# Residual rows loaded into freed operand space, the order of seven products, and which bank is copied

## The chip, the core and the metric

One core of a Trainium2 chip runs the whole program; nothing is exchanged with other cores. The metric is device time in microseconds (us) of one execution. Engines are named as in the profile: PE does the matmuls, DVE and ACT the elementwise work, SP issues every DMA of the stages told of here, from one queue, in the order in which the issues stand.

## What is computed

A decoder block on x of 1024 tokens by 1024 channels, all float32: two token mixers in parallel (dilated attention and retention), their gated sum through an output projection, a residual add, and then the channel mixer, which is where most of the change lies:

```python
x = x + y @ w_out[l]
xn2 = rmsnorm(x, norm2_g[l])
x = x + jnp.square(jax.nn.relu(xn2 @ w_up[l])) @ w_down[l]
```

The up projection is 1024 by 4096, the down projection 4096 by 1024. The residual rows are the x of the second line, which the last line adds.

## The kernel before

**Split operands.** Every operand is held as a high and a low half (`split`, line 317: ACT rounds a copy to the high half, DVE subtracts it to get the low half), and each product of 128 by 128 by 512 is three matmuls: high by high, low by high, high by low (`Pipe.group`, line 218).

**Seven products.** The input projections, the up projection and the down projection use a seven-product scheme in the place of eight block products. The names N1 to N7 stand for the seven products. Several add up in one PSUM bank: N1 and N2 in bank "a", N6, N7 and N4 in bank "b" (which ACT first fills with minus the result of N1), N5 and N3 in bank "d" (`BANK`, line 253). A product of the up projection is 12 matmuls, one of the down projection 6.

**Order of the up projection.** `strassen_order` (line 256) writes the order out. In a unit j (256 of the 4096 columns) it is N6, N5, then N1 of unit j+2, N7, N2 of unit j+2, N4, N3; the last three units have less of j+2 in them. Because N7 and N4 add to the same bank, what N7 left there has to be read before N4 starts. `product` (line 368) does that: after N7, ACT copies bank b into the tile u3 (line 395), DVE subtracts bank d from it (line 396), and u3 is the block's result. After N3, DVE subtracts from bank d what ACT had copied after N6 (line 401).

**What becomes of the results.** `result` (line 1099) applies Relu and Square on ACT, forms four more sums on DVE (line 1116), and `put_operand` (line 1121) splits each of the seven operands of the down projection and writes it to DRAM (`h_d<-hs`, 512 KB each, seven in a unit, from four buffers). The weights of a unit come in two loads of 512 KB (`raw<-in_w_up`), are split into four pieces A to D, and a raw buffer is loaded again when its last piece has been split: the first of the two when piece B is (`wl2` or `wl3` in the names), the second when piece C is (`wl5`).

**The down projection.** Its units are (chunk c of 512 rows of w_down, pair t of token tiles), 32 in all, four to a chunk. `load_rows` (line 1135) brings a unit's seven operands from `h_d` into space that had held an operand of the up projection: two pieces, high and low, of 896 KB each; three units are in flight. `load_sums` (line 1145) loads the residual rows of two token tiles (Y, 512 KB each): Y0 and Y4 while the up projection still runs, the six others, Y1 to Y7, after it. `down` (line 1151) does one product of 6 matmuls, and DVE adds its bank to Y (line 1173). In a unit, N7 may start only when DVE has subtracted bank b, as N6 left it, from Y.

**Weights of a chunk.** Four loads of 512 KB (raw0 to raw3) into four buffers, then seven splits with four sums between them (`add_chunks`, line 137; the sums are line 153). In the even chunks they go to the weight buffers and the space of operand N2; in the odd chunks to buffer 3 and the space of the operands N7, N4 and N3.

**What sets the order.** PE runs in the order of the program. The instructions of the other engines are placed by a scheduler when the program is built, and each engine and the SP queue then run theirs strictly in that order: an instruction that waits holds up all behind it.

Of the kernel before, what the change touches and what calls it, by code (L numbers as in the profile page):

```python
# [10 lines left out]
F = mybir.dt.float32  # L11
# [257 lines left out]
def hybrid_block(ctx: ExitStack, tc: tile.TileContext, a: dict, out: bass.AP):  # L269
# [87 lines left out]
    for nb in range(2):  # L357
        for u in range(4):
# [2 lines left out]
    W.add_units("up", [a["w_up"][j] for j in range(NU)])  # L361
    NC = FF // 512
    W.add_chunks("dn", [[a["w_down"][c, i] for i in range(4)] for c in range(NC)],
                 [{"N1": 0, "N2": 1, "N3": 2, "N5": "N2a", "N7": "N2b", "N6": 5, "N4": 4},
                  {"N1": "N7a", "N2": "N7b", "N3": 3, "N5": "N4a", "N7": "N4b", "N6": "N3a", "N4": "N3b"}])
    pipe = Pipe(nc)

    def product(tag, j, name, unit, operands, pu, result):

        u = unit.setdefault(j, {})  # L370
        bank = BANK[name]
        fresh = bank not in u
# [12 lines left out]
        if name == "N1":  # L385
            u["b"] = ms.tile([P, 512], F, name="ms")
            nc.scalar.activation(u["b"], ps, AF.Copy, scale=-1.0)
        elif name == "N2":
            result(j, 0, lo, ps)
        elif name == "N6":  # L390
            u["u2"] = pu().tile([P, 512], F, name="u2")
            nc.scalar.activation(u["u2"], ps, AF.Copy)
        elif name == "N7":
            u["u3"] = pu().tile([P, 512], F, name="u3")
            nc.scalar.activation(u["u3"], ps, AF.Copy)  # L395
# [510 lines left out]
    with ExitStack() as ph:  # L906
# [15 lines left out]
            nc.sync.dma_start(t, src)  # L922
            return t

        ES, e1 = None, ExitStack()
        work = [(d, cs) for d in range(KT) for cs in halves()]
        gates = [loaded(pm2, sg_d[0, d, :, cs], "s0") for d, cs in work[:3]]
        waiting = [(place, n) for n, place in enumerate(oS)]
        for d in range(KT):
            ua, = W.take(1)  # L930
            uh, ul = W[ua]
            for cs in halves():
                if len(gates) < len(work):
                    e, es = work[len(gates)]
                    gates.append(loaded(pm2, sg_d[0, e, :, es], "s0"))
                sga = gates[2 * d + (cs.start > 0)]
                pp = ms.tile([P, 512], F, name="ms")
                pipe.step(pp, [(uh[:, k * P:(k + 1) * P], ul[:, k * P:(k + 1) * P], oaS[k][0][:, cs], oaS[k][1][:, cs])
                               for k in range(SLOTS)], {SLOTS - 1: lambda: W.free(ua)} if cs.start else None)
                nc.vector.tensor_tensor(sga, sga, pp, op=OP.mult)  # L940
                nc.sync.dma_start(pa_d[d, :, cs], sga)
                if ES is None and not pipe.due:
                    ret.close()
                    ext = pool(body, "ext", 3, "right")
# [46 lines left out]
        e1.close()  # L991


    W.more = pool(body, "more", 1, "right")
# [90 lines left out]
    with ExitStack() as ph:  # L1085
# [3 lines left out]
        def temps():  # L1089

            nonlocal up_pool
            if up_pool is None:
                assert pipe.slot > last_turn
                norm2.close()
                load_sums(pool(sumst, "y0", 1), 0)
                up_pool = pool(ph, "p26", 2)
            return up_pool

        def result(j, f, cs, src):
# [10 lines left out]
            held[j, q] = r  # L1110
            if q != "u2":
                put_operand(j, {"q11": "N1", "q12": "N2", "u3": "N4"}[q], r)
                return
            q11, q12, q21, q22 = (held.pop((j, q)) for q in ("q11", "q12", "u2", "u3"))
            for name, x, y in (("N5", q22, q21), ("N7", q21, q11), ("N6", q11, q22), ("N3", q12, q11)):
                nc.vector.tensor_tensor(x, x, y, op=OP.add)
                put_operand(j, name, x)

        held = {}

# [24 lines left out]
        def load_sums(from_, t):  # L1145

            for r in (t, t + 4):
                Y[r] = from_.tile([P, D], F, name=f"Y{r}")
                nc.sync.dma_start(Y[r], y_d[r * P:(r + 1) * P, :])

        def down(u, name):

# [26 lines left out]
        for j, name in strassen_order(NU):  # L1179
            product("up", j, name, unit, OP7, temps, result)  # L1180
            if j == NU - 1:
                if name == "N1":
                    load_rows(0)
                if name in ("N2", "N7", "N4", "N3"):
                    xh, xl = (x.rearrange("p a b -> p (a b)") for x in OP7[name])
                    for i, part in enumerate("ab"):
                        W.places[name + part] = xh[:, 1024 * i:1024 * i + 1024], xl[:, 1024 * i:1024 * i + 1024]
                    W.free(("place", name))
                if name == "N6":
                    load_rows(1)  # L1190
                if name == "N5":
                    load_rows(2)
                if name == "N7":
                    down(0, "N1")
                if name == "N4":
                    down(0, "N2")


    with ExitStack() as ph:
        y1 = pool(ph, "y1", 1)  # L1200
        for t in range(1, 4):
            load_sums(y1, t)
# [106 lines left out]
```

## Time and profile before

| | |
|---|---|
| median of 3 runs | 2282.35 us (2281.9 to 2283.52) |
| the profiled execution, its own time | 2283.06 us |
| its span, first to last instruction | 2281.3 us |
| granted PE clock, mean | 0.995 |
| PE busy in the span | 2230.9 us, 98% |
| DVE, ACT busy | 1340.2 us, 983.9 us |
| moved by DMA | 353.53 MB, 155 GB/s on average |

The up projection runs from about 1640 to 1963 us of the span, the down projection from there to the end, with a few products of each mixed at the seam. In the views, a row of a timeline is start, duration, engine, line, operation and, in brackets, how long the engine had been idle and what ended that. A line that says L223 is any matmul, L319 or L318 any split, so tile names tell more than lines: `wl<-raw,wh` is the split of a weight piece, `hs` that of an operand on its way to DRAM, `Y` a residual row tile. Names that begin with x (`xl<-raw,xh`) are weight pieces too, where they lie in space that had been an operand's.

### The profile page before, as it was taken

Reading aid. Unit: us, or ns where it says so; the run is one execution under the profiler, and the core shown is the slowest. Engines: PE = TensorE matmul, PEld = TensorE weight load, DVE = VectorE, ACT = ScalarE, POOL = GpSimd, SP = SyncE. Lnnn points to the kernel's source line nnn. Section 1 sums busy time; section 2 is a strip of 40 time slices with the busy share of each in tenths; the row PEclk is TensorE's granted clock in tenths of the full one; section 3 lists DMA queues with packets and bytes.
Section 4 is the critical chain, followed back from the end, with each engine's and each line's share of the span. In section 5 each row is a group of like instructions: output and inputs, shape, how many; then the busy total and the mean of one; then the engine's idle time right before and its main releaser. Section 6 shows DMA issues by size and latency. Waiting matters only on the chain.

```text
span 2281.3 us, 29992 instructions
## 1 busy us (share of the span) xinstructions
PE 2230.9 (98%) x10868; PEld 1910.0 (84%) x10868; DVE 1340.2 (59%) x2588; ACT 983.9 (43%) x2166; POOL 103.2 (5%) x148
## 2 busy tenths in 40 slices
PE   8999999999999999999999999999899999599999
PEld 7999999998888888878888888888787787488887
DVE  6444545355544445557777852453877777677774
ACT  6444435345333333435555633122666666322220
POOL 1111111110000000000000000000000000000000
PEclk9999999999999999999999999999999999799999
DMA  4313132222233333263433484564378889966655
GB/s 148 98 52 109 59 94 90 86 84 98 88 111 111 111 111 108 101 189 112 121 120 102 129 294 153 167 190 145 115 219 238 246 249 273 324 236 260 237 221 201
DMA packets 288805, 353.53 MB, mean 155 GB/s; under 512 B 14609, under 2 KB 215441, under 8 KB 288658
## 3 DMA queue, kind: packets, MB, share of 16 engines
q1 hardware_dynamic: 288658, 351.63, 48.5%
q8 instruction: 85, 1.39, 0.2%
q14 instruction: 62, 0.51, 0.1%
HBM read 229.84 MB, written 121.73 MB: 154 GB/s over the span
## 4 chain that ended last, share of the span: by engine, by line
PE 81%; DVE 6%; ACT 5%; DMA 4%; issue 3%; POOL 0%; SPq 0%; POOLq 0%; DVEq 0%; ACTq 0%
PE mm L223 53%; PE ms L223 22%; DMA raw<-in_w_up 2%; DVE wl L319 1%; PE ms L603 1%; PE ms L583 1%; ACT wh L318 1%; PE tr L659 1%; DVE xl L319 1%; ACT u L1108 1%; DVE hs L319 1%; ACT hs L318 1%; PE ms L596 1%; ACT u L1109 1%; PE ms L819 1%
## 5 line engine op out<-in xcount | busy, mean ns | idle before, releaser
L223 PE MATMUL mm<-wh,xh 128*128 128x384 f32 (+1 forms) x1280 | 502.9, 393 | 0.1
L319 DVE TENSOR_TENSOR wl<-raw,wh 128x1024 fp32r<-128x1024 f32 (+2 forms) x274 | 296.5, 1088 | 306.7 <-ACT wh L318 305.6
L223 PE MATMUL mm<-wh,xl 128*128 128x384 f32 (+1 forms) x1280 | 460.0, 359 | 2.3 <-DVE xl L319 2.3
L223 PE MATMUL mm<-wl,xh 128*128 128x384 f32 (+1 forms) x1280 | 459.0, 359 | 0.0
L318 ACT ACTIVATE wh<-raw 128x1024 fp32r<-128x1024 f32 (+2 forms) x274 | 258.5, 950 | 315.6 <-PE ms L223 75.2
L223 PE MATMUL mm<-xl,wh 128*128 128x512 f32 x848 | 309.3, 389 | 1.7 <-DVE xl L319 1.7
L223 PE MATMUL mm<-xh,wh 128*128 128x512 f32 x848 | 309.5, 389 | 0.0
L223 PE MATMUL mm<-xh,wl 128*128 128x512 f32 x720 | 280.1, 389 | 0.0
L223 PEld LDWEIGHTS mm<-wh,xl 128*128 128x128 f32 x1280 | 241.1, 188 | 24.7 <-DVE xl L319 3.3
L223 PEld LDWEIGHTS mm<-wh,xh 128*128 128x128 f32 x1280 | 242.1, 189 | 21.0 <-DVE Y L1173 0.6
L223 PEld LDWEIGHTS mm<-wl,xh 128*128 128x128 f32 x1280 | 243.0, 190 | 19.2 <-DVE wl L319 0.4
L223 PE MATMUL ms<-xh,wh 128*128 128x512 f32 x604 | 240.0, 397 | 6.5 <-ACT u L395 4.5
L223 PE MATMUL ms<-xl,wh 128*128 128x512 f32 x604 | 235.4, 390 | 0.7 <-DVE xl L319 0.7
L223 PE MATMUL ms<-xh,wl 128*128 128x512 f32 x604 | 235.3, 390 | 0.0
L223 PEld LDWEIGHTS mm<-xl,wh 128*128 128x128 f32 x848 | 159.2, 188 | 35.0 <-DVE xl L319 2.2
L223 PEld LDWEIGHTS mm<-xh,wh 128*128 128x128 f32 x848 | 159.2, 188 | 33.0
L223 PEld LDWEIGHTS mm<-xh,wl 128*128 128x128 f32 x720 | 135.1, 188 | 28.1
L223 PEld LDWEIGHTS ms<-xh,wh 128*128 128x128 f32 x604 | 113.5, 188 | 36.9 <-ACT u L395 10.5
L223 PEld LDWEIGHTS ms<-xh,wl 128*128 128x128 f32 x604 | 113.4, 188 | 24.0
L223 PEld LDWEIGHTS ms<-xl,wh 128*128 128x128 f32 x604 | 113.5, 188 | 22.9 <-DVE xl L319 1.0
L590 ACT ACTIVATE pr<-s,acc 128x128 f32<-128x128 f32 (+1 forms) x96 | 43.1, 449 | 148.6 <-DVE acc L588 122.1
L1173 DVE TENSOR_TENSOR Y<-Y,ms 128x512 f32<-128x512 f32 x96 | 65.8, 686 | 61.8 <-PE ms L223 61.7
(206 smaller groups left out, 3281.8 us busy)
## 6 DMA issues: line engine op xcount, KB each, us to landing
h_d<-hs SPq DMA_DIRECT2D x112, 512.0 KB, 5.2
xh<-h_d SPq DMA_DIRECT2D x32, 896.0 KB, 5.4
xl<-h_d SPq DMA_DIRECT2D x32, 896.0 KB, 7.1
raw<-in_w_att SPq DMA_DIRECT2D x48, 384.0 KB, 3.9
raw<-in_w_up SPq DMA_DIRECT2D x32, 512.0 KB, 4.3
raw<-in_w_down SPq DMA_DIRECT2D x32, 512.0 KB, 6.0
sg_d<-sg SPq DMA_DIRECT2D x32, 256.0 KB, 2.0
raw<-in_w_rqk_q SPq DMA_DIRECT2D x16, 512.0 KB, 3.7
```

The costliest lines, as they stand in the source:

```text
L223: self.nc.tensor.matmul(ps, x, y, start=start, stop=stop, skip_group_check=not first)
L318: nc.scalar.activation(dst_h, src, AF.Copy)
L319: nc.vector.tensor_tensor(dst_l, src, dst_h.bitcast(F), op=OP.subtract)
L583: nc.tensor.matmul(sp[:, :n], qT[:, b * P:(b + 1) * P], kT[:, k0:k0 + n], start=True, stop=True)
L590: nc.scalar.activation(st["p"][:, :n], s[:, :n], AF.Exp, bias=acc[:, b, DH:DH + 1], accum_out=acc[:, b, DH + 1:DH + 2])
L596: nc.tensor.transpose(tp[:, j * P:(j + 1) * P], st["p"][:, j * P:(j + 1) * P], ident)
L603: nc.tensor.matmul(po[:, :DH], st["t"][:, j * P:(j + 1) * P], V[:, k0 // P + j, :], start=(j == 0), stop=(j == nk - 1))
L659: nc.tensor.transpose(pt[:, j, :], qk[:, j, :], ident)
L819: nc.tensor.matmul(sp[:, :P], kT[:, f], qT[:, f], start=(f == 0), stop=(f == 1))
L1108: nc.scalar.activation(r, src, AF.Relu)
L1109: nc.scalar.activation(r, r, AF.Square)
L1173: nc.vector.tensor_tensor(Y[r][:, ns], Y[r][:, ns], ps, op=op)
```

## The change

Three edits, which go together.

- **Order.** N3 now stands ahead of N4 in each unit, wherever the seven-product order is used.
- **Bank.** ACT copies bank d after N5 instead of bank b after N7; after N7, DVE subtracts that copy from bank b, straight from PSUM. The operands that need only u2 and u3 are summed and written after N3, the two that need N4's block after N4.
- **Space.** The six tiles Y1 to Y7 lie where the operands N7, N4 and N6 of the up projection had been (the pool `ext`, closed when the last product has been issued), and three of an odd chunk's weight pieces lie behind them (y1a to y1c); three more (w1a to w1c) lie in the space of the up projection's temporaries, where Y had been. The rows of a unit go to the space of operands N1, N5 and N3, not N1, N6 and N5.

```diff
-        order += [(j, "N4"), (j, "N3")]
+        order += [(j, "N3"), (j, "N4")]
...
-                 [{"N1": 0, "N2": 1, "N3": 2, "N5": "N2a", "N7": "N2b", "N6": 5, "N4": 4},
-                  {"N1": "N7a", "N2": "N7b", "N3": 3, "N5": "N4a", "N7": "N4b", "N6": "N3a", "N4": "N3b"}])
+                 [{"N1": 0, "N2": 1, "N3": 2, "N5": "n2a", "N7": "n2b", "N6": 5, "N4": 4},
+                  {"N1": "y1a", "N2": "y1b", "N3": "y1c", "N5": 3, "N7": "w1a", "N6": "w1b", "N4": "w1c"}])
...
-        elif name == "N7":
+        elif name == "N5":
             u["u3"] = pu().tile([P, 512], F, name="u3")
             nc.scalar.activation(u["u3"], ps, AF.Copy)
-            nc.vector.tensor_tensor(u["u3"], u["u3"], u["d"], op=OP.subtract)
+        elif name == "N7":
+            nc.vector.tensor_tensor(u["u3"], ps, u["u3"], op=OP.subtract)
             result(j, 1, hi, u["u3"])
...
-            q11, q12, q21, q22 = (held.pop((j, q)) for q in ("q11", "q12", "u2", "u3"))
-            for name, x, y in (("N5", q22, q21), ("N7", q21, q11), ("N6", q11, q22), ("N3", q12, q11)):
-                nc.vector.tensor_tensor(x, x, y, op=OP.add)
-                put_operand(j, name, x)
+            sums = {"u2": (("N5", "u3", "u2"), ("N7", "u2", "q11"), ("N6", "q11", "u3")),
+                    "q12": (("N3", "q12", "q11"),)}.get(q, ())
+            for name, x, y in sums:
+                nc.vector.tensor_tensor(held[j, x], held[j, x], held[j, y], op=OP.add)
+                put_operand(j, name, held[j, x])
...
-                for i, x in enumerate(OP7[("N1", "N6", "N5")[u % 3]]):
+                for i, x in enumerate(OP7[("N1", "N5", "N3")[u % 3]]):
...
+        exts.close()
+        y1 = pool(sumst, "y1", 1, "right")
+        places = {t: [y1.tile([P, D], F, name=f"Y{r}") for r in (t, t + 4)] for t in (1, 3, 2)}
+        for t in range(1, 4):
+            load_sums(t, places[t])
```

The SP queue around the loads of Y, before: the last row loads of the third unit ahead (xh_91, xl_92), the four weight loads of chunk 2 (raw0 to raw3) and the six of Y.

```order
L1142 DMA xh_91<-h_d_89 128x1792
L176 DMA raw0_17726<-in_w_down 128x1024
L176 DMA raw2_17733<-in_w_down 128x1024
L176 DMA raw1_17731<-in_w_down 128x1024
L176 DMA raw3_17735<-in_w_down 128x1024
L1149 DMA Y1_17741<-y_d_90 128x1024
L1149 DMA Y5_17743<-y_d_90 128x1024
L1149 DMA Y2_17745<-y_d_90 128x1024
L1149 DMA Y6_17747<-y_d_90 128x1024
L1149 DMA Y3_17749<-y_d_90 128x1024
L1149 DMA Y7_17751<-y_d_90 128x1024
L1142 DMA xl_92<-h_d_89 128x1792
```

And with the change, from the last weight load of chunk 1 on:

```order
L176 DMA raw3_17707<-in_w_down 128x1024
L1152 DMA Y1_17713<-y_d_90 128x1024
L1152 DMA Y5_17714<-y_d_90 128x1024
L1152 DMA Y2_17717<-y_d_90 128x1024
L1152 DMA Y6_17718<-y_d_90 128x1024
L1152 DMA Y3_17715<-y_d_90 128x1024
L1152 DMA Y7_17716<-y_d_90 128x1024
L176 DMA raw0_17758<-in_w_down 128x1024
L176 DMA raw2_17765<-in_w_down 128x1024
L176 DMA raw3_17767<-in_w_down 128x1024
L176 DMA raw1_17763<-in_w_down 128x1024
L1145 DMA xh_91<-h_d_89 128x1792
```

The loads of Y have moved ahead of the four weight loads of chunk 2, and the row loads (xh_91, and xl_92 behind it) have moved behind those four.

DVE in one unit of the up projection, before, from the subtraction after N3 (u2 from bank d) on; q11 and q12 are the results of N2 and N4, raw0 and raw1 the unit's weights with the four sums of line 121, and wl2 is the split of piece B, behind which SP loads raw1 again:

```order
L401 TENSOR_TENSOR u2_16823<-mm_16825,u2_16823 128x512
L121 TENSOR_TENSOR raw1_16722<-raw1_16722,raw0_16720 128x512
L121 TENSOR_TENSOR raw1_16722<-raw1_16722 128x512
L1116 TENSOR_TENSOR u3_16865<-u3_16865,u2_16823 128x512
L1116 TENSOR_TENSOR u2_16823<-u2_16823,q11_16582 128x512
L319 TENSOR_TENSOR wl2_16966<-raw1_16722,wh2_16965 128x1024
L319 TENSOR_TENSOR hs_16946<-u3_16865,hs_16946 128x512
L319 TENSOR_TENSOR hs_16951<-u2_16823,hs_16951 128x512
L1116 TENSOR_TENSOR q11_16582<-q11_16582,u3_16865 128x512
L1116 TENSOR_TENSOR q12_16917<-q12_16917,q11_16582 128x512
L319 TENSOR_TENSOR hs_16956<-q11_16582,hs_16956 128x512
L319 TENSOR_TENSOR hs_16961<-q12_16917,hs_16961 128x512
```

And with the change, up to the same split:

```order
L319 TENSOR_TENSOR hs_16921<-u3_16838,hs_16921 128x512
L319 TENSOR_TENSOR hs_16926<-u2_16823,hs_16926 128x512
L1119 TENSOR_TENSOR q11_16582<-q11_16582,u3_16838 128x512
L121 TENSOR_TENSOR raw0_16720<-raw0_16720 128x512
L121 TENSOR_TENSOR raw0_16720<-raw0_16720,raw1_16722 128x512
L319 TENSOR_TENSOR hs_16931<-q11_16582,hs_16931 128x512
L319 TENSOR_TENSOR hs_16950<-q12_16947,hs_16950 128x512
L121 TENSOR_TENSOR raw1_16722<-raw1_16722,raw0_16720 128x512
L1119 TENSOR_TENSOR q12_16947<-q12_16947,q11_16582 128x512
L121 TENSOR_TENSOR raw1_16722<-raw1_16722 128x512
L319 TENSOR_TENSOR hs_16955<-q12_16947,hs_16955 128x512
L319 TENSOR_TENSOR wl2_16966<-raw1_16722,wh2_16965 128x1024
```

The five splits hs and the two sums of q11 and q12, of which six stood behind the split of piece B before, now all stand ahead of it.

DVE at the seam, before: the splits and sums of chunk 1's weights from raw1 on, and the first two uses of Y1.

```order
L319 TENSOR_TENSOR xl_12940<-raw1_17661,xh_12939 128x1024
L319 TENSOR_TENSOR wl3_17714<-raw2_17663,wh3_17713 128x1024
L153 TENSOR_TENSOR raw0_17626<-raw0_17626,raw3_17665 128x1024
L153 TENSOR_TENSOR raw3_17665<-raw3_17665,raw2_17663 128x1024
L319 TENSOR_TENSOR xl_12942<-raw0_17626,xh_12941 128x1024
L153 TENSOR_TENSOR raw2_17663<-raw2_17663,raw0_17626 128x1024
L319 TENSOR_TENSOR xl_12942<-raw3_17665,xh_12941 128x1024
L153 TENSOR_TENSOR raw1_17661<-raw1_17661,raw2_17663 128x1024
L319 TENSOR_TENSOR xl_98<-raw2_17663,xh_97 128x1024
L319 TENSOR_TENSOR xl_98<-raw1_17661,xh_97 128x1024
L1173 TENSOR_TENSOR Y1_17741<-Y1_17741,mm_17768 128x512
L1173 TENSOR_TENSOR Y1_17741<-Y1_17741,ms_17775 128x512
```

And with the change:

```order
L319 TENSOR_TENSOR y1bl_17728<-raw1_17703,y1bh_17727 128x1024
L319 TENSOR_TENSOR y1cl_17730<-raw2_17705,y1ch_17729 128x1024
L153 TENSOR_TENSOR raw0_17624<-raw0_17624,raw3_17707 128x1024
L1176 TENSOR_TENSOR Y1_17713<-Y1_17713,mm_17784 128x512
L153 TENSOR_TENSOR raw3_17707<-raw3_17707,raw2_17705 128x1024
L319 TENSOR_TENSOR wl3_17739<-raw0_17624,wh3_17738 128x1024
L153 TENSOR_TENSOR raw2_17705<-raw2_17705,raw0_17624 128x1024
L319 TENSOR_TENSOR w1al_17747<-raw3_17707,w1ah_17746 128x1024
L153 TENSOR_TENSOR raw1_17703<-raw1_17703,raw2_17705 128x1024
L319 TENSOR_TENSOR w1bl_17749<-raw2_17705,w1bh_17748 128x1024
L1176 TENSOR_TENSOR Y1_17713<-Y1_17713,ms_17791 128x512
L319 TENSOR_TENSOR w1cl_17751<-raw1_17703,w1ch_17750 128x1024
```

The two uses of Y1 now stand among those splits and sums, the second ahead of the last split.

More of the change, by code (lines that the diff above doesn't have):

```diff
@@ L991, in hybrid_block @@
         e1.close()
-    W.more = pool(body, "more", 1, "right")
+    W.more = more
     OP7 = {"N1": before[0], "N2": before[1], "N3": XS[1, 1], "N5": XS[0, 1], "N4": XS[1, 0], "N7": XS[0, 0],
@@ L1094, in temps @@
                 norm2.close()
-                load_sums(pool(sumst, "y0", 1), 0)
+                y0 = pool(sumst, "y0", 1)
+                load_sums(0, [y0.tile([P, D], F, name=f"Y{r}") for r in (0, 4)])
                 up_pool = pool(ph, "p26", 2)
@@ L1143, in load_rows, with load_sums @@
                     rows[u].append(x.rearrange("p (o k q) -> p o k q", o=7, k=2))
[L1145 to L1149, printed above, removed]
+        def load_sums(t, places):
+            for r, place in zip((t, t + 4), places):
+                Y[r] = place
+                nc.sync.dma_start(place, y_d[r * P:(r + 1) * P, :])
         def down(u, name):
@@ L1183, in hybrid_block @@
                     load_rows(0)
[L1184 to L1185 removed]
+                if name == "N2":
+                    parts = [x.rearrange("p a b -> p (a b)") for x in OP7[name]]
                     for i, part in enumerate("ab"):
[L1187 to L1189 removed]
+                        W.places["n2" + part] = [x[:, 1024 * i:1024 * i + 1024] for x in parts]
+                    W.free(("place", "n2"))
+                if name == "N5":
                     load_rows(1)
[L1191 to L1192 removed]
                 if name == "N7":
                     down(0, "N1")
[L1195 removed]
+                if name == "N3":
+                    load_rows(2)
                     down(0, "N2")
+        exts.close()
[3 more added lines that the diff above has]
+            load_sums(t, places[t])
+        for x in "abc":
+            W.places["y1" + x] = [y1.tile([P, UW], R, name=f"y1{x}{i}") for i in "hl"]
+        W.free(("place", "y1"))
     with ExitStack() as ph:
[L1200 to L1202 removed]
+        w1 = pool(ph, "w1", 1)
+        for x in "abc":
+            W.places["w1" + x] = [w1.tile([P, UW], R, name=f"w1{x}{i}") for i in "hl"]
+        W.free(("place", "w1"))
         for u in range(len(units)):
```

6 lines of the change are left out of this document (3 added, 3 removed).

## The prediction

> **What bounds the kernel now.** The page comes first. PE is busy for 98% of the span, and the slices show the one place where it isn't: slice 35, about 1939 to 1996 us, where the granted clock falls too.
>
> ```profile
> span 2281.3 us, 29992 instructions
> PE 2230.9 (98%) x10868; PEld 1910.0 (84%) x10868; DVE 1340.2 (59%) x2588; ACT 983.9 (43%) x2166; POOL 103.2 (5%) x148
> PE   8999999999999999999999999999899999599999
> PEclk9999999999999999999999999999999999799999
> ```
>
> PE's timeline there shows one wait of 22.64 us, ahead of N7 of the down projection's second unit. The matmuls behind it start 0.43 us apart until 1990.51, and then 0.23: eleven steps, 4.86 us in the place of 2.5, so 2.4 us more.
>
> ```profile
> 1962.62 0.39 PE L223 MATMUL mm<-wh,xl 128*128 128x512 f32 x1
> 1985.65 0.79 PE L223 MATMUL ms<-xh 128*128 128x512 f32 x1 [22.64 <-DVE Y L1173]
> 1990.08 0.60 PE L223 MATMUL mm<-wl,xh 128*128 128x512 f32 x1
> 1990.51 0.41 PE L223 MATMUL mm<-wh,xl 128*128 128x512 f32 x1
> ```
>
> The chain of waits, DVE's and ACT's timelines and that of the SP queue say what PE waits for: DVE's subtraction from Y1, which waits for the load of Y1. That load was issued at 1977.14, behind four weight loads of chunk 2 (5.39 us at SP), whose buffers come free only when DVE has split chunk 1: ten pieces from 1964.62 to 1976.26, 1.16 each.
>
> ```profile
> 1973.91 2.36 DVE xl L319 x2
> 1976.29 0.33 SPq L176
> 1977.61 7.95 DMA Y<-y_d
> 1985.65 2.93 PE ms L223 x6
> ...
> 1964.62 1.23 DVE L319 TENSOR_TENSOR xl<-raw,xh 128x1024 fp32r<-128x1024 f32 x1 [1.76 <-ACT xh L318]
> 1973.83 2.43 DVE L319 TENSOR_TENSOR xl<-raw,xh 128x1024 fp32r<-128x1024 f32 x2
> 1984.31 0.69 DVE L1173 TENSOR_TENSOR Y<-Y,mm 128x512 f32<-128x512 f32 x1 [8.05 <-DMA Y<-y_d]
> ...
> 1938.42 0.63 ACT L318 ACTIVATE hs<-q 128x512 fp32r<-128x512 f32 x1 [2.44 <-DMA h_d<-hs]
> ...
> 1903.30 0.35 SPq L176 DMA_DIRECT2D raw<-in_w_down  x1
> 1903.90 5.32 SPq L1126 DMA_DIRECT2D h_d<-hs  x4
> 1931.64 11.53 SPq L1126 DMA_DIRECT2D h_d<-hs  x6
> 1971.70 5.39 SPq L176 DMA_DIRECT2D raw<-in_w_down  x4
> 1977.14 3.89 SPq L1149 DMA_DIRECT2D Y<-y_d  x6
> ```
>
> But the transfers themselves are full by then: the windows show a DMA share of 1.02 to 1.11 up to 1970, at 320 to 374 GB/s.
>
> ```profile
> 1940.00:1950.00 10.00, 8.46 (x36) 6.67 (x37) 9.64 (x11) 7.65 (x12) 0.00 (x0) 1.00 1.02 320
> 1950.00:1960.00 10.00, 9.85 (x44) 7.84 (x43) 9.69 (x16) 3.71 (x7) 0.00 (x0) 1.00 1.04 374
> 1960.00:1970.00 10.00, 3.00 (x14) 2.15 (x12) 7.43 (x8) 5.77 (x7) 0.00 (x0) 0.83 1.11 374
> ```
>
> A smaller loss lies in the up projection. In each unit N4 waits for ACT's copy of bank b: here its first matmul starts 0.61 us behind the one before it and the second 0.34 behind that, where 0.23 each is the rule, so 0.50 us, and 6.5 us in 13 units. The copy (line 395) is late because ACT first waited for a weight load. The load's own issue recurs every 19.65 us (nine units from 1706.71 to 1883.52), where PE needs seven products of 2.72 us, 19.04. So a ring of load, split and sums sets the pace, not the copy.
>
> ```profile
> 1850.40 0.39 PE L223 MATMUL mm<-xh,wl 128*128 128x512 f32 x1
> 1851.01 0.50 PE L223 MATMUL ms<-xh,wh 128*128 128x512 f32 x1 [0.22 <-ACT u L395]
> 1851.35 0.39 PE L223 MATMUL ms<-xl,wh 128*128 128x512 f32 x1
> ...
> 1848.47 2.01 ACT L318 ACTIVATE wh<-raw 128x1024 fp32r<-128x1024 f32 x2 [0.59 <-DMA raw<-in_w_up]
> 1850.39 0.58 ACT L395 ACTIVATE u<-ms 128x512 f32<-128x512 f32 x1
> ...
> 1706.71 4.20 DMA raw<-in_w_up
> 1844.40 4.04 DMA raw<-in_w_up
> 1883.52 4.27 DMA raw<-in_w_up
> 1995.02 2.72 PE mm L223 x12
> ```
>
> **Bank and order.** The copy keeps its cost (0.58 us) and moves behind N5; N3, which overwrites bank d, comes three products later (8.2 us), so the copy is covered. The subtraction from bank b stays one DVE instruction (0.69 us, as other DVE reads of PSUM at 1984.31), and N4 now stands two products behind N7, N2 and N3, 5.4 us. The waits at N4 should go: 6.5 us of PE's time. But they are not 6.5 us of the result. PE would only come to the seam earlier, and wait there for DVE and the transfers, which go at the ring's pace.
>
> **The ring.** Two kinds of unit alternate in the new order. From the issue of a weight load to the next: 4.04 for the load, 1.0 for ACT's half of the split, then on DVE two pieces (1.14 to the next start, and 1.22) and sixteen small ones.
>
> ```profile
> 1843.16 1.22 DVE L319 TENSOR_TENSOR wl<-raw,wh 128x1024 fp32r<-128x1024 f32 x1
> 1844.30 1.28 DVE L319 TENSOR_TENSOR hs<-u,hs 128x512 fp32r<-128x512 f32 x2
> 1845.50 0.68 DVE L1116 TENSOR_TENSOR q<-q,u 128x512 f32<-128x512 f32 x1
> ...
> DMA to landing us min/median/max: 4.0/4.3/6.3
> ```
>
> The small ones take 0.61 each (1.28 for two, 0.60 to the next), 9.8 together; all of it 17.2. DVE's waits for Relu, Square and the high halves come on top; counting them through the order at ACT's durations (0.6 each) I get 2.7 in one kind and 1.5 in the other, where the subtraction after N3 stands one place earlier. That is 19.9 and 18.7, 19.3 on average, 0.35 less than 19.65. The six instructions that stood in the load's shadow stand ahead of it now, and five stores are issued shortly before each load, so I take a quarter of a microsecond for a slower load (4.3, the median, for 4.04) and keep 0.1 for a unit: 1.2 us in 12 units. The ends: PE's own 19.04 would give 7.3, a unit of 20.05 would cost 4.8.
>
> **The seam, first stretch.** From the first weight load of chunk 0 (1903.30) to the landing that frees ACT at 1938.42, 35.1 us pass. By the order, that store is the first of the six issued from 1931.64 on. Twelve stores, four weight loads and two row pieces are in it: 16 times 0.524 MB and 2 times 0.918, 10.2 MB, 291 GB/s. In the new order the four stores of the unit before stand ahead of the load; 2.1 MB less are 7.2 us less. That holds if the transfers set this stretch, which their share supports; if data are late instead, nothing is gained, and at most 8.4 (four at 2.1 us).
>
> **The seam, second stretch.** From that store's landing to Y1 there are now 11 stores, 5 row pieces, 8 weight loads and Y1, 15.1 MB, 45.9 us to DVE's first use at 1984.31. With the change there are 11 stores, 4 row pieces, 4 weight loads and Y1: 12.1 MB. At 356 GB/s, the mean of the three windows, 33.9 us; at 374, 32.2; at 328, the mean of the whole stretch, 36.7. So Y1 comes 12 us earlier. But PE resumes only when DVE has done the second use of Y1, and nine pieces of chunk 1 now stand ahead of that. Their first, raw1, lands three loads before Y1 (1.57 MB, 4.4 us): 33.9 less 4.4, ACT's 1.0, nine pieces of 1.16, two uses of 0.7: 42.3 us, where it is 47.2 now (1938.42 to 1985.65). 4.9 us are gained. The loads behind wait with SP, but nothing on PE needs them first.
>
> [...]
>
> **Behind the seam.** The rows of unit 3 now stand behind the weight loads of chunk 2, the last of which waits for the last split of chunk 1, 1.2 us after PE has resumed. PE needs these rows 10.7 us after it has resumed (1996.38, half of the pair at 1995.02). The landing of a low piece took 9.3 us:
>
> ```profile
> xl<-h_d SPq DMA_DIRECT2D x5, 896.0 KB, 9.3
> ```
>
> With 0.5 for the issue, 11.0 against 10.7: 0.5 us as a guess, from nothing to 2. Nothing on PE's side changes later, since PE is busy without a gap from there on.
>
> The slow clock stays: the wait that is left is some 20 us, as PE comes 6 us earlier. The Trainium skill, "TensorE: Matmul & The Clock Gate" (What's actually happening), halves the clock after an idle window of about 3.4 us, for as long; the trace agrees with its 0.43 us steps. By that rule a shortened wait, or rows late by over 3.4 us, would still be charged 2.4 us; by the sum none is saved either.
>
> **The sum.** 7.2 + 4.9 + 1.2 - 0.5 = 12.8 us. From the profiled execution's 2283.06 (its span and 1.76 around it; 0.7 above the median of the runs): 2270.3 us.
>
> **The rivals.**
>
> *The whole wait goes.* Y comes ahead of chunk 2, and if the transfers weren't the limit, PE would lose neither the 22.8 nor the 2.4 us, nor the 6.5: 2251. Against it stands the full DMA share from 1940 to 1970. Chance 0.07; something between, at faster transfers, 2252 to 2262: 0.08.
>
> *The ring takes it back.* If DVE's extra work ahead of each weight load makes every unit 20.05 us, 4.8 are lost; and if the first stretch waits for data, its 7.2 don't come: 4.9 - 4.8 - 0.5, about nothing, 2283.5. For it: six instructions have left the load's shadow. Against: DVE idles behind ACT and the load. This is also the case that the change doesn't do what it says: N4's waits go and nothing is gained. 0.11.
>
> *Slower.* One mechanism: the weight load of each unit of the up projection queues behind the five stores issued in the 8 us ahead of it. At 6.3 us for a load, the most seen, a unit takes 19.3 + 2.26, 1.9 more than now; 12 units lose 23, the seam gives 11.6: 2294. It decides from a load of about 5.3 us on. Against it: the median is 4.3, with stores about as many. 0.06.
>
> **Chances and range.** The forecast, 2270.3, has 0.68. Its own range: down to 2262, where the ring falls to PE's pace (6.1 more) and the second stretch runs at 374 (1.7); up to 2281, where the ring costs 4.8 (6.0 more), the second stretch runs at 328 (2.8) and the rows cost 2 (1.5). That alone would leave out 0.32, so the range reaches on to 2284, which takes in the case of the ring, and down to 2256, which takes in some 0.05 of what lies between: 0.16 is left out. What can be told from no change is 0.2%, 4.6 us, so 2277.8 to 2286.9. Faster: 0.68 less 0.03 for the top of its own range, 0.15 of the two faster cases, and 0.05 of the ring's 0.11, where half of it is spent: 0.85. Same: the other 0.09. Slower: 0.06.
>
> **What would show it.** Right: no idle time at N4 with line 395 or 397 as its end; weight loads of the up projection 19.2 to 19.6 us apart; PE's one long wait still ahead of N7 of the second unit, about 20 us, ended by DVE's use of Y1, with chunk 1's splits and sums ahead of it on DVE; six loads of Y ahead of chunk 2's on SP; a DMA share near 1 up to the landing of Y1. Wrong: PE's wait under 10 us, or over 1 us a unit at any product of the up projection, or a second long wait ahead of N1 of unit 3 for its rows.

## The result

The changed kernel takes 2305.45 us (median of 4 runs, 2301.12 to 2310.31) where the kernel before, on the same chip, takes 2282.12 (2281.55 to 2283.52): 1.0102 times as long, with a 95% interval of 1.0081 to 1.0123. It is slower by 23 us; the forecast was 2270.3.

### The profile page after: what moved, and what is told of

The parts are those of the page before. It is cut to its first block, busy times and chain, and to the rows that moved or that the text cites. A ratio compares the mean times of both kernels' runs of the same rounds, so it can differ in the third digit from the quotient of the medians.

```text
span 2304.7 us, 29956 instructions
## 1 busy us (share of the span) xinstructions
PE 2236.1 (97%) x10868; PEld 1913.1 (83%) x10868; DVE 1339.1 (58%) x2588; ACT 994.1 (43%) x2166; POOL 103.0 (4%) x148
## 4 chain that ended last, share of the span: by engine, by line
PE 78%; DVE 8%; DMA 6%; ACT 4%; issue 3%; SPq 0%; POOL 0%; POOLq 0%; DVEq 0%; ACTq 0%
PE mm L223 52%; PE ms L223 20%; DMA raw<-in_w_up 3%; DVE hs L319 2%; PE ms L604 1%; PE ms L584 1%; ACT wh L318 1%; DVE wl L319 1%; DMA raw<-in_w_down 1%; PE tr L660 1%; DMA pa_d<-s 1%; DVE raw L121 1%; DVE xl L319 1%; DVE q L1119 1%; PE ms L597 1%
## 5 line engine op out<-in xcount | busy, mean ns | idle before, releaser
L223 PE MATMUL mm<-xh,wh 128*128 128x512 f32 x848 | 312.0, 392 | 14.8 <-ACT ms L387 14.8
L223 PEld LDWEIGHTS ms<-xl,wh 128*128 128x128 f32 x604 | 113.5, 188 | 23.4 <-DVE xl L319 1.0
```

The costliest lines, as they stand in the source:

```text
L223: self.nc.tensor.matmul(ps, x, y, start=start, stop=stop, skip_group_check=not first)
```

## The profile after

The page first: the span is 23.4 us longer, PE is 5 us busier and 97% busy. The dip in slice 35 is still there, and slice 18, about 980 to 1037 us, has lost a tenth.

```profile
span 2304.7 us, 29956 instructions
PE 2236.1 (97%) x10868; PEld 1913.1 (83%) x10868; DVE 1339.1 (58%) x2588; ACT 994.1 (43%) x2166; POOL 103.0 (4%) x148
PE   8999999999999999989999999999999999699999
```

PE's waits in the changed kernel, two of the groups by what ended them (total, times, longest). The longest wait for Y is shorter than the 22.64 us of before, and there is no group for the copy of line 395. But ten waits for L387 are new (the copy of N1's bank, for which N2 waits). That copy now stands on ACT right behind the split of a weight piece, as L395's did before: a wait of the same kind stands at N2 now, 14.8 us in all, where N4's were 4.5 in thirteen. New too is one wait of 6.5 us for a load of the retention, far ahead of the up projection (at 1009.03 below).

```profile
PE ms L223 <- DVE Y L1176: 17.9, 3, 16.1
PE mm L223 <- ACT ms L387: 14.8, 10, 3.1
```

To see where 23.4 us arise, the same instructions are found in both timelines. Before:

```profile
1311.25 0.50 PE L223 MATMUL ms<-xh,wh 128*128 128x512 f32 x1 [1.17 <-DVE St L866]
1636.52 0.63 PE L1014 MATMUL tr<-ident,xn 128*128 128x128 f32 x4 [2.80 <-DVE x L1034]
```

And in the changed kernel, PE's timeline, with SP's row of the first weight loads of the down projection at the end:

```profile
1009.03 1.20 PE L820 MATMUL ms<-rqT,rkT 128*128 128x128 f32 x4 [6.45 <-DMA rkT<-rqk_d]
1317.00 0.50 PE L223 MATMUL ms<-xh,wh 128*128 128x512 f32 x1 [1.17 <-DVE St L867]
1358.03 0.47 PE L223 MATMUL ms<-xh,wh 128*128 128x512 f32 x1 [1.75 <-DVE s L941]
1644.86 0.63 PE L1016 MATMUL tr<-ident,xn 128*128 128x128 f32 x4 [2.76 <-DVE x L1036]
1868.41 0.50 PE L223 MATMUL mm<-xh,wh 128*128 128x512 f32 x1 [2.46 <-ACT ms L387]
2007.80 0.80 PE L223 MATMUL ms<-xh 128*128 128x512 f32 x1 [16.08 <-DVE Y L1176]
2020.04 0.50 PE L223 MATMUL mm<-wh,xl 128*128 128x512 f32 x1 [1.04 <-DMA xl<-h_d]
...
1931.31 1.51 SPq L176 DMA_DIRECT2D raw<-in_w_down  x2
```

| stretch of the span | before, us | changed, us | more |
|---|---|---|---|
| start to the first output projection (1311.25; 1317.00) | 1311.25 | 1317.00 | 5.75 |
| to the last transposes ahead of the up projection (1636.52; 1644.86) | 325.27 | 327.86 | 2.59 |
| to the first weight load of the down projection (1903.30; 1931.31) | 266.78 | 286.45 | 19.67 |
| to PE's resumption after its long wait (1985.65; 2007.80) | 82.35 | 76.49 | -5.86 |
| to the end (2281.3; 2304.7) | 295.65 | 296.9 | 1.25 |

**The up projection, +19.67.** The chain of waits runs through the weight load of each unit. Before, the first load of a unit took 4.0 to 4.3 us; here ten that the chain shows from 1679.85 on, of which four are copied, take 5.59 on average (4.65 to 6.77), and the issue recurs every 21.05 us (ten units from 1679.85 to 1890.39), not 19.64.

```profile
1679.85 5.13 DMA raw<-in_w_up
1700.97 6.77 DMA raw<-in_w_up
1722.59 4.65 DMA raw<-in_w_up
...
1890.39 4.66 DMA raw<-in_w_up
```

SP's timeline shows a candidate. Both weight loads of a unit are issued in one row of 2.08 us, the second 1.7 behind the first, with seven stores ahead and none between; the last of the seven has been issued 1.1 to 1.4 us before the first load. Before, the two loads were 7.6 us apart (1746.25 and 1753.88) with four stores between, and the last store ahead of the first load was issued 5.1 us before it. So two things have changed around that load: a second load right behind it, and stores close ahead of it.

```profile
1743.25 2.08 SPq L176 DMA_DIRECT2D raw<-in_w_up  x2
1746.57 16.34 SPq L1129 DMA_DIRECT2D h_d<-hs  x7
```

Before, the same queue:

```profile
1737.93 3.21 SPq L1126 DMA_DIRECT2D h_d<-hs  x3
1746.25 0.35 SPq L176 DMA_DIRECT2D raw<-in_w_up  x1
1746.85 5.66 SPq L1126 DMA_DIRECT2D h_d<-hs  x4
1753.88 0.35 SPq L176 DMA_DIRECT2D raw<-in_w_up  x1
```

**The retention's load, +5.75.** The chain around 1000 us: DVE's last sum of an input projection (L747), the store of it (L751) on SP, and right behind that the load of the first keys, which PE waits for. Before, that load was issued at 999.61; here the store stands ahead of it on SP, and its data are late, since N4's block is now the last of a unit and N3's the one before.

```profile
1002.59 0.69 DVE sg L747
...
1003.30 0.32 SPq L751
...
1003.66 5.23 DMA rkT<-rqk_d
...
1009.03 1.20 PE ms L820 x4
```

**The output projections, +2.59.** PE waits 1.75 us for a gate's product (DVE, L941), which waits for a gate's load. On SP an up projection's weight load now stands among the loads and stores of the gates, at 1336 us. Before, none was there (the first was issued at 1529.53): the fourth weight buffer is opened earlier in the program now.

```profile
1336.12 0.42 SPq L176 DMA_DIRECT2D raw<-in_w_up  x1
```

**The seam, -5.86.** SP's and DVE's timelines. The six loads of Y are indeed ahead of chunk 2's, and Y1 is there when DVE first uses it (1999.66, no idle time ahead). But three weight loads of chunk 1 are issued only from 1985.70 on, behind stores that wait for DVE. DVE then idles 9.41 us for the first of them, and reaches the second use of Y1 at 2007.07, behind eight more splits and sums. Nor are the transfers full all the way: from 1960 to 1970 us the DMA share is 0.76, at 211 GB/s.

```profile
1985.70 5.68 SPq L176 DMA_DIRECT2D raw<-in_w_down  x3
1991.42 3.70 SPq L1152 DMA_DIRECT2D Y<-y_d  x6
2003.81 5.43 SPq L176 DMA_DIRECT2D raw<-in_w_down  x4
...
1995.89 1.23 DVE L319 TENSOR_TENSOR y1bl<-raw,y1bh 128x1024 fp32r<-128x1024 f32 x1 [9.41 <-ACT y1bh L318]
1999.66 0.68 DVE L1176 TENSOR_TENSOR Y<-Y,mm 128x512 f32<-128x512 f32 x1
2007.07 0.68 DVE L1176 TENSOR_TENSOR Y<-Y,ms 128x512 f32<-128x512 f32 x1
```

## The experiments

The theory formed from these views: three losses, each from the place of one DMA on SP's queue (the retention's load, the up projection's second weight load, the load into the fourth buffer), and a seam that gains little. The kernel before ran beside the experiments: 2282.84 us beside the first four, 2283.51 beside the next four, 2282.10 beside the last four. Ratios are to that kernel.

### The old order in the input projections

```diff
-        order += [(j, "N3"), (j, "N4")]
+        order += [(j, name) for name in last]
...
-        for j, name in strassen_order(NIN):
+        for j, name in strassen_order(NIN, ("N4", "N3")):
```

(and in `product`, the old bank where the tag is "in").

> The changed kernel, but with the old order and the old bank in the input projections; the new ones in the up projection and the new space stay. Theory: the wait of 6.45 us for the first retention keys at 1009 us, and the slow clock behind it, come from the last store of the input projections, which now waits for N4 and holds the SP queue; both go, the up projection starts 8.3 us earlier, near 1636.5, and the time is 2297. Rival: the wait comes with the new space (the pool under it is opened at another place), and the time stays at 2305.

Measured: 2298.76 us, 1.0073 (1.0056 to 1.0090). PE's wait for the keys is 0.64 us:

```profile
1005.88 0.68 PE L825 MATMUL ms<-rqT,rkT 128*128 128x128 f32 x4 [0.64 <-DMA rkT<-rqk_d]
1351.35 0.47 PE L223 MATMUL ms<-xh,wh 128*128 128x512 f32 x1 [2.80 <-DVE s L946]
```

So the first loss is of the order in the input projections; the trace shows it, while by time alone the two intervals overlap. The up projection starts 5.1 us earlier than in the changed kernel, not 8.3, because the wait for the gates is still there (2.80 us here): that is another cause.

### The second weight load two stores later

The two raw buffers of a unit change their turn, and the load into the one of piece C is recorded ahead of N3, pinned on SP (kept at that place of the program) behind what stands there by then:

```diff
+    def release(self):
+        if self.held:
+            self.used.add(self.held.pop(0))
+            self.pinned = True
+            self.load()
+            self.pinned = False
...
         for j, name in strassen_order(NU):
+            if name == "N3":
+                W.release()
```

> The changed kernel, but the second weight load of each unit of the up projection stands two stores behind the first, and not next to it. Theory: the two loads, issued 1.74 us apart, share the transfer rate, which is why the first takes 5.6 us and not 4.1; apart, it takes 4.1 to 4.3 again, a unit 19.5 to 19.7 us, and the time is 2287 (18 less). Rival A: the load is slow because seven stores stand ahead of it; it stays at 5.3 to 5.8 and the time at 2305. Rival B: the load gets faster, but DVE's order takes the gain back, and a unit stays at 21.

Measured: 2293.39 us, 1.0047 (1.0032 to 1.0062), about 12.6 us less than the changed kernel by the ratios. The first loads of the units take 3.6 to 4.3 us, but for one of 5.33:

```profile
1743.31 3.74 DMA raw<-in_w_up
1763.36 4.27 DMA raw<-in_w_up
1771.01 5.24 DMA raw<-in_w_up
...
1750.43 0.57 SPq L185 DMA_DIRECT2D raw<-in_w_up  x1
1754.73 5.74 SPq L1148 DMA_DIRECT2D h_d<-hs  x5
1763.36 0.35 SPq L185 DMA_DIRECT2D raw<-in_w_up  x1
```

Five stores still stand ahead of the first load (1754.73), and it is as fast as before, so the count of stores is not what made it slow. But the run doesn't separate the two things that had changed. The second load is 4.5 to 8.7 us away again, and the last store now ends 2.2 to 3.3 us ahead of the first load, not 1.1 to 1.4. The second loads, issued right behind two stores and with no load within 12 us behind them, took 4.6 to 5.5 us here. The run with the bank alone, below, says more. A unit takes 19.80 us on average (first loads at 1683.36 and, ten units later, at 1881.33). The theory's 19.5 to 19.7 is missed by a little, because in every third unit the second load has become the late one (1771.01). The time is 6 us above the theory's 2287; in the table's terms the up projection to the first load of the down projection takes 271.98 us (1647.12 to 1919.10), 14.5 less.

### The order and the bank alone

The kernel before with the first two edits, its old space and its old place of the Y loads.

> The kernel before with the new order, the new bank and the sums that follow from them, but with the old space and the old place of the Y loads. Theory: both losses are of the order alone, 8.3 at the input projections and 18 in the up projection; the seam gains nothing of the new space, so 2308 to 2311. Rival: the order also gave what was gained at the seam (5.9 us), and the time is 2303.

Measured: 2301.85 us, 1.0087 (1.0072 to 1.0103): the rival's number. The wait for the keys is 6.35 us, the weight loads take 4.61 to 6.59, so the two losses are of the order (taken together with the bank). And PE's long wait is 16.34 us without the new space, where it is 16.08 with it:

```profile
2001.60 0.79 PE L223 MATMUL ms<-xh 128*128 128x512 f32 x1 [16.34 <-DVE Y L1174]
```

From the first weight load of the down projection (1925.63) to PE's resumption it takes 75.97 us without the new space, and 76.49 with it. So what the seam seemed to gain in the changed kernel came with the order and the bank; that PE merely arrives later, with the slower units, is likely but not shown. With the new order, the new space bought nothing that can be measured (the two intervals overlap).

### The space alone

The new space with the old order, bank and sums.

> The kernel before with the new space alone: Y1 to Y7 are loaded ahead of chunk 2, the old order, bank and sums stay. Theory: no loss at the input projections, units of 19.64 us as before; the seam gains what it gained in the changed kernel, 5.9 less 1.2 behind it: 2277.5. Rival A: with the old order more stores are late, and the loads of Y only change place with the wait for chunk 1: 2282. Rival B: the forecast's reckoning of the seam holds when the units aren't stretched: 12 us less, 2270.

Measured: 2281.26 us, 0.9992 (0.9983 to 1.0001): not to be told from no change by time, though the profiled execution (2278.27) was the fastest of ten. Its trace says why little comes of it. The long wait for Y is gone, and PE waits for row loads in its place:

```profile
1350.88 0.47 PE L223 MATMUL ms<-xh,wh 128*128 128x512 f32 x1 [1.65 <-DVE s L940]
1971.69 0.77 PE L223 MATMUL mm<-wh,xh 128*128 128x512 f32 x1 [8.91 <-DMA xh<-h_d]
```

From 1637.71 to the end (2276.1) it takes 638.4 us, 6.4 less than before (644.8); the theory's 5.9 less 1.2 is near. (By the median the kernel gains only 1.6 us, so this execution shows it at its best.) But the gates' wait is there, and 1.9 us of the gain are lost between the first output projection and the up projection.

### The fourth buffer's load behind the output projections

The kernel with the new space alone, and:

```diff
         dma = self.nc.sync.dma_start(raw[:, :self.src[n].shape[1]], self.src[n])
+        if b == self.RAW and self.first:
+            self.first = False
+            self.pin(dma)
```

> The kernel of the new space alone, but the first weight load of the up projection into the fourth weight buffer stays behind the output projections on the SP queue (with the new space it stands among the gate loads and stores, at 1329 us). Theory: that load is what delays the gate loads; PE's wait of 1.65 us at 1351 us goes, and the time is 2 us less than with the new space, 2279. Rival: the gates wait for the places they are loaded to, and nothing changes: 2281.

Measured: 2279.83 us, 0.9981 (0.9972 to 0.9991). The wait for the gates is gone, and the stretch from the first output projection (1313.91) to the up projection (1639.31) takes 325.40 us, as before the change (325.27). The trace shows the third loss's cause; the time agrees with the theory, but the intervals with and without the pin touch.

### All three repairs

> The changed kernel with all three repairs at once: the old order in the input projections, the second weight load of a unit two stores behind the first, and the load into the fourth buffer behind the output projections. Theory: the three losses are separate and add up: 2293.4 of the kernel with the later load, less 6.7 of the old order in the input projections, less 2.3 of the pinned load: 2284. Rival A: they share one cover, and the sum is smaller: 2288. Rival B: with units as short as before, the new space gives at the seam what it gave with the old order, 6.4 us less than before: 2277.

Measured: 2284.10 us, 1.0000 (0.9991 to 1.0009). The theory's sum, on its number: the three losses are separate, and with them repaired the whole change is worth nothing. PE resumes 349.69 us after the start of the up projection, where it was 349.13:

```profile
1986.34 0.80 PE L243 MATMUL ms<-xh 128*128 128x512 f32 x1 [16.09 <-DVE Y L1202]
```

### The bank alone

The kernel before, and in `product`:

```diff
-        elif name == "N7":
+        elif name == "N5":
             u["u3"] = pu().tile([P, 512], F, name="u3")
             nc.scalar.activation(u["u3"], ps, AF.Copy)
-            nc.vector.tensor_tensor(u["u3"], u["u3"], u["d"], op=OP.subtract)
+        elif name == "N7":
+            nc.vector.tensor_tensor(u["u3"], ps, u["u3"], op=OP.subtract)
             result(j, 1, hi, u["u3"])
```

> The kernel before with the other bank alone: ACT copies bank d after N5, DVE subtracts that copy from bank b after N7; order, sums and space stay. Theory: the 0.5 us at N4 of each unit go, but the weight loads stay 19.6 us apart, so PE waits as long at the seam or elsewhere, and the time stays within 1 us of 2282.8. Rival A: all 6.5 us come: 2276. Rival B: DVE reads bank b later than ACT did, N4 waits longer and the time is 2288.

Measured: 2278.30 us, 0.9974 (0.9964 to 0.9984). The theory falls: the first weight loads of the units are issued 19.15 us apart (eleven units between the two rows of SP here), near PE's own pace of 19.04 and not at 19.64, and most of rival A's gain arrives. The last row is PE's long wait; the two rows at 1762.30 and 1768.76, and the landing time below them, are of the second load of one unit:

```profile
1665.04 0.35 SPq L176 DMA_DIRECT2D raw<-in_w_up  x1
...
1762.30 5.09 SPq L1127 DMA_DIRECT2D h_d<-hs  x4
1768.76 0.35 SPq L176 DMA_DIRECT2D raw<-in_w_up  x1
...
DMA to landing us min/median/max: 5.4/5.4/5.4
...
1875.66 0.34 SPq L176 DMA_DIRECT2D raw<-in_w_up  x1
...
1980.38 0.80 PE L223 MATMUL ms<-xh 128*128 128x512 f32 x1 [23.34 <-DVE Y L1174]
```

Why the units got shorter is only in part shown. For the most part the ring of before did not run through PE: the chain of waits goes from load to load over ACT and DVE alone in ten units of twelve, from 1844.40 to 1883.52 for instance, and over the copy and PE in the two from 1746.25 to 1785.60. But moving the copy shortens that ring. In twelve units ACT now waits 3.9 us for DVE's subtraction of u3, where it waited 12.8 before, and the first loads take 3.5 to 4.2 us, where they took 4.0 to 4.3. How much each of the two gives is not shown. PE resumes 344.82 us after 1635.56, 4.3 less than before; the wait at the seam is longer by 0.7.

This run also bears on the slow loads of the changed kernel. Its second loads are issued 1.4 us behind the last of four stores, with no other load within 8 us on either side, and the eleven whose landing the trace shows take 5.0 to 6.2 us (5.4 on average), nearly as long as the pairs (5.59). Its first loads, 3.5 to 3.9 us behind a store, are the fast ones. The kernel before has it too: its second loads, 1.1 to 1.4 us behind four stores, took 4.2 to 6.3 us. So stores close ahead of a load are enough to make it slow; what the second load beside it adds, no run isolates.

### Chunk 1's weights from another queue

The kernel with the three repairs, and:

```diff
+        queue = self.nc.gpsimd if n in self.aside else self.nc.sync
-        dma = self.nc.sync.dma_start(raw[:, :self.src[n].shape[1]], self.src[n])
+        dma = queue.dma_start(raw[:, :self.src[n].shape[1]], self.src[n])
...
+    W.aside = range(len(W.src) + 4, len(W.src) + 8)
```

> The kernel with the three repairs, and the four weight loads of chunk 1 of the down projection issued from POOL's queue, where nothing stands ahead of them. Theory: PE's long wait at the seam ends when chunk 1's weights have been split, and three of their loads stand on the SP queue behind stores that wait for DVE, some 8 us after their buffers are free; from POOL they land earlier and the wait of 16 us falls to 8 to 10: 6 to 8 us less than with the three repairs alone. Rival: the transfers are full there (share 1.06 to 1.10), so the loads only change places with stores and rows, and the time moves by less than 2 us.

Measured: 2278.48 us, 0.9976 (0.9967 to 0.9985), 5.6 less than with the repairs alone. The four loads are issued from 1945.38 to 1960.57; from SP the last three came at 1964.48 to 1969.92. PE's long wait is 13.09 us, and it now stands one unit earlier in the down projection, since DVE's use of Y has moved too. The theory's size of the wait was too low, its gain nearly right: the place on SP counted, the transfers did not forbid it.

```profile
1945.38 0.69 POOL L188 DMA_DIRECT2D raw<-in_w_down  x1 [314.72 <-DVE xl L341]
1960.57 0.54 POOL L188 DMA_DIRECT2D raw<-in_w_down  x1 [7.72 <-DVE wl L341]
```

### Versions with the old order

Three kernels without the new order, from the edits above. The first has the new space, the new bank and the pinned load:

> The new space and the new bank with the old order and sums, the load into the fourth buffer behind the output projections. Theory: what the bank gave alone (5.2 us) and what the space gave with that load (3.7) add up: 2274.6 where the kernel before takes 2283.5. Rival A: with units at PE's pace, 19.07 us, more stores are late at the seam and the space gives nothing: 2278.

Measured: 2272.79 us, 0.9960 (0.9948 to 0.9973), where the theory's 2274.6 beside 2283.5 is 0.9961. The gains of bank and space add up.

The same with chunk 1's weights from POOL's queue:

> The same, and the four weight loads of chunk 1 from POOL's queue. Theory: 5.6 us less again, as with the three repairs: 2269. Rival: here PE waits at the seam for rows and not for chunk 1's weights (8.4 us for the rows of unit 1 in the kernel with the new space), so earlier weight loads only delay the rows: 2274 or more.

Measured: 2270.53 us, 0.9944 (0.9931 to 0.9956), the fastest of all: 11.6 us less than before, and 1.6% less than the changed kernel. PE's one long wait is 12.43 us (at 1959.80). As a ratio the theory's 2269 is 0.9937 and the rival's 2274 is 0.9958, so it is nearer to the theory. But it is only 2.3 us below the kernel without the other queue, and the two intervals overlap.

The bank and POOL's queue, in the old space (the kernel holds the pin of the fourth buffer's load too, which the expectation doesn't name):

> The kernel before with the new bank, and the four weight loads of chunk 1 from POOL's queue; old order, old space. Theory: the long wait is for Y1, whose load stands behind chunk 2's four, which wait for chunk 1's splits; chunk 1's weights some 8 us earlier bring Y1 earlier by 5 to 6: 2273. Rival: transfers set the stretch, 2278.

Measured: 2274.35 us, 0.9966 (0.9952 to 0.9979). The theory's 2273 is 0.9954, the rival's 2278 is 0.9976: it lies between, and the interval holds both, so whether POOL's queue is worth anything in the old space stays open. Beside the kernel just above, which has the pin as well, the new space is worth 3.8 us here, though the two intervals touch.

### The sums behind N4

The changed kernel, and in `result`:

```diff
-            sums = {"u2": (("N5", "u3", "u2"), ("N7", "u2", "q11"), ("N6", "q11", "u3")),
-                    "q12": (("N3", "q12", "q11"),)}.get(q, ())
+            sums = {"q12": (("N5", "u3", "u2"), ("N7", "u2", "q11"), ("N6", "q11", "u3"), ("N3", "q12", "q11"))}.get(q, ())
```

> The changed kernel, but all four sums of a unit, and their stores, stand behind N4, as they stood behind the last product before. Theory: the two weight loads of a unit still stand side by side on the SP queue behind seven stores, so the load takes 5.5 us, a unit 21, and the time is 2303 to 2306. Rival (the forecast's own reckoning of DVE): the three sums that stand ahead of the split of piece B cost the time; without them a unit is back at 19.6 and the time 2288.

Measured: 2311.29 us, 1.0124 (1.0110 to 1.0137). The loads are still issued in pairs and take 4.3 to 7.9 us; a unit takes 21.85. The rival is out. As a ratio it is 0.2% above the changed kernel, which the theory had not, but the two intervals overlap.

```profile
1680.04 5.86 DMA raw<-in_w_up
...
1830.65 7.92 DMA raw<-in_w_up
...
1898.54 2.08 SPq L176 DMA_DIRECT2D raw<-in_w_up  x2
```

## Why the prediction was wrong

It forecast 12.8 us less and got 23.4 more in the profiled execution, 36.2 apart. By the rows of the table: 8.3 ahead of the up projection that it didn't have; 20.9 in the up projection (19.7 more for the 1.2 less that it gave); 6.2 at the seam (5.9 gained for 12.1); 0.75 behind it.

**The ring, the largest miss: a load of 4.3 us.** The walk through DVE's order was good: without the load it gave 19.3 - 4.04 = 15.26 us for a unit, and the trace shows 21.05 - 5.59 = 15.46. The term that failed is "a quarter of a microsecond for a slower load": it is 1.55 us slower, 5.59 for 4.04. The rival "slower" had the load at 6.3 and a price of 23 us for the units, with 5.3 as the point of decision; it had the right term, and a chance of 0.06. Its mechanism, stores issued shortly ahead of the load, has the runs on its side: seven stores (it counted five) end 1.1 to 1.4 us ahead, and loads that close behind a store take 5.0 to 6.2 us with no other load near. What no run separates is how much the second load, 1.7 us behind, adds. Its sum, 2294, was still 11 us short, since it had neither loss ahead of the up projection and gave the seam 11.6. The order of DVE quoted ahead of the prediction ends at the split of piece B. The next big split in the same order is piece C's, and behind it the second load: one look at SP's order would have shown the two loads side by side, right behind seven stores, where four stores had stood between.

**"So a ring of load, split and sums sets the pace, not the copy."** The chain of waits bears this out for the kernel before, in ten units of twelve: it goes from load to load without PE. What failed is the step from there to a price. The prediction gave the 6.5 us at N4 nothing of the result, as if taking the copy away left the ring as it was; with the bank alone the units fall from 19.64 to 19.15 us and 5.2 us come off the time. Whether the changed kernel holds this gain under its slower loads isn't shown: with the three repairs its units still take 19.9 us (first loads at 1672.81 and, eleven units later, at 1891.95).

**The input projections.** The prediction did not look there, since PE is fully busy in them. The loss is not inside but at their end, where the next stage's load stands behind their last store. In the trace with the old order the wait falls from 6.45 to 0.64 us.

**The new space as an edit without a price.** The pool of the fourth weight buffer is opened earlier, and so a weight load of 512 KB moved to 1336 us, some 200 us ahead of the next of its kind (1540.44), in among the gates' loads, and PE waits 1.75 us there. That was to be seen in SP's order.

**The seam.** The kind was right: PE's one long wait stays ahead of N7 of the second unit, at 16.08 us, ended by DVE's use of Y1 behind chunk 1's splits and sums, with Y ahead of chunk 2. The size was not. "That holds if the transfers set this stretch" was the condition of 7.2 us, and the 4.9 were reckoned at transfer rates too; it does not hold. The DMA share falls to 0.76 on the way, three loads of chunk 1 stand on SP behind stores that wait for DVE, and moving four loads to another queue is worth 5.6 us. That the seam gave 5.9 at all is luck as far as the forecast's reason goes, since the order and the bank give as much in the old space (75.97 us for 76.49). With the old order the freed wait turns into one for rows, 8.91 us. The rows of unit 3, a guess of 0.5, show a wait of 1.04.

**What held.** No wait at N4 for L395 or L397 is left (its sign of being wrong, over 1 us a unit at some product, shows at N2: 14.8 us in ten waits), the slow clock stays (matmuls 0.43 us apart behind the wait), and behind the rows of unit 3 PE is busy to the end, as before.

What stays open: what the second load adds to a load that has stores close ahead, whether the sums behind N4 cost anything beside the changed kernel, and whether row loads or stores hold the last 12 us of the seam in the fastest kernel.

## What to carry to other kernels

A change of order has to be read on the DMA queue as well as on the engines: which stores and loads a load now stands close behind, and which store now stands ahead of the next stage's first load. Where an edit is used in several stages, the end of each is a place of its own. And where a ring of waits sets the pace, walk it once more with the edit in it before giving the edit no price: an edit made for another wait can shorten the ring itself.

## What the runs showed of the hardware

In four kernels of this case (before, changed, the later load, the bank alone), a weight load of 512 KB in the up projection took 3.4 to 4.3 us (once 5.33) when the last 512 KB store ahead of it on the queue had been issued 2.2 us or more before and no other load followed within 4 us. It took 4.2 to 6.8 us when a store had been issued 1.4 us or less before it, with a second load 1.7 us behind (4.4 to 6.8) or without one (4.2 to 6.3). The number of stores ahead did not decide: with five, the last of them 2.2 to 3.3 us away, the load was fast.

Behind PE's wait of 16.08 us the matmuls started 0.43 us apart for 4.9 us (2007.80 to 2012.66); behind the wait of 1.75 us at 1358.03 they started 0.23 us apart, the first step of 0.31 aside.
